# Meta tokens' values and the meta queries' turned block by one product of the whole array from masked copies

## The chip, the cores and the metric

One Trainium2 chip; the kernel runs on one of its cores. The metric is the device time of one execution in microseconds (us), as the median of the runs. On the core work TensorE (PE in the rows; its weight loads are PEld), VectorE (DVE), ScalarE (ACT) and GpSimd (POOL); SP issues the DMAs of the weights.

## What is computed

Two layers of a bidirectional encoder trunk. In front of the 256 tokens of the sequence stand 16 learned meta tokens. In each layer the input is normalised and projected; four token mixers of four heads each (A windowed attention with sinks, B rotary attention, C differential attention, D a gated linear recurrence in both directions) run side by side; their outputs are gated, merged, and a feed-forward block follows. Cut to the parts around the change:

```python
for l in range(DEPTH):
    u = rms_norm(h, ln_mix[l])
    (aq, ak, av, bq, bk, bv, cq, ck, cv, dq, dzf, dzb, di, dg, gz) = split_in(u @ w_in[l])
    y_a = windowed_sink_attention(aq, ak, av, attn_sink[l], bias_a)
    y_b = axial_rope_attention(rms_norm(bq, qk_norm_q[l]), rms_norm(bk, qk_norm_k[l]), bv, row, col, key_ok)
    y_c = differential_attention(cq, ck, cv, lam, bias_c, key_ok, diff_subnorm[l], lam_init)
    y_d = hgrn2_bidirectional(dq, dzf, dzb, di, dg, lb_all[0, l], lb_all[1, l], valid, hgrn_out_norm[l])
    gate = sigmoid(gz).reshape(Bn, L, N_BRANCH, D_MODEL)
    merged = sum(gate[:, :, n] * (y @ w_branch[l, n]) for n, y in enumerate((y_a, y_b, y_c, y_d)))
    h = h + merged @ w_out[l]
    u = rms_norm(h, ln_ffn[l])
    h = h + (silu(u @ w_ffn_gate[l]) * (u @ w_ffn_up[l])) @ w_ffn_down[l]
return rms_norm(h, ln_final)[:, META_END:]
```

Every mixer's output is, per head, weights (softmax or decayed scores) times values, over the meta tokens and the sequence. In the second layer only the sequence's outputs are needed, so the meta tokens are keys and values there, but not queries.

## The kernel before

Activations lie with features on the 128 partitions and the 272 tokens (16 meta, 256 of the sequence) along the free dimension. A projection to 128 features is a `block`: 24 matmuls (eight slices of the input, three products each of a value split in a high and a low fp32r part; L291 to L293) into one PSUM tile of the tag `pmm`. The weights stream through SP's queue, and ACT and DVE split each of them in two (L276, L277). The small products of the mixers are in f32, into PSUM tiles of the tag `pat`, of which there are four.

PE's order is written out by hand (`tc.manual_schedule`): the loop over `ORDER` runs one block after the other, and between blocks `catch_up` runs one step that was put off (`later`), and `advance` runs pieces of two generators, `branch_d` (mixer D) and `softmax_stream` (C, then B, then A). The order of the other engines is planned by the framework from the program's order and its own estimates of when operands are ready; each engine then runs its queue in order. A tile of a pool waits until the buffer that it gets is free.

What the change touches:
- `values` (L410) makes, from the projected values of a branch (features on partitions), `vn`, the sequence's values with tokens on the partitions (transposes, L417), and `vm`, the 16 meta tokens' values for four heads, each head on its own 32 partitions. For `vm` (L422 to L426) each head has a product of 64 contracted rows, 32 stationary columns (the meta tokens' columns, padded to 32) and 64 moving columns (`C_E`, an identity repeated in both halves). L427 masks the result. `take` (L938) puts `values` off to the next `catch_up`; for branch B `take_b` is put off first.
- `turn_meta` (L463) runs in layer 0 for C, B and A, one unit of the stream after the weights of the meta queries were made. Those lie as one tile of 128 partitions: 32 rows for each of the four heads, 272 keys along the free dimension. L467 turns the two halves of the sequence's keys; L470 turns the block of the meta keys, head by head, by four products of 32 rows and 32 columns with a piece of the identity.
- `mix` (L432) uses `vm` and the turned blocks. L443 and L437 are its products.
- L723 and L735 are the small products of `branch_d`; L402, L566, L393, L817 and L826 are small products that follow the block of `aq0` in layer 0; L460 is the transpose of the sequence queries' meta keys, by way of a copy in a tile of the tag `pmeta` (two buffers).
- `prep_small` (L158) works out four small parameters; `load_bias("a")` (L239 to L246) fills and masks a bias table from POOL's queue.

Of the kernel before, what the change touches and what calls it, by code (L numbers as in the profile page):

```python
# [8 lines left out]
F32 = mybir.dt.float32  # L9
# [3 lines left out]
ALU = mybir.AluOpType  # L13
AX = mybir.AxisListType

P = 128
# [4 lines left out]
T = META + SEQ  # L21
# [9 lines left out]
SWAP16 = list(range(16, 32)) + list(range(16))  # L31


C_ID, C_E, C_COS, C_SIN, C_SEL, C_RM, C_CM, C_EPS, C_ONE, C_WIDTH = (
    0, 128, 192, 464, 736, 738, 740, 742, 744, 872)
M_WIDTH = 5 * 32
Q_LNM, Q_LNF, Q_LNO, Q_SINK, Q_SINKM, Q_QK, Q_SUB, Q_OUT, Q_LAM, Q_LB, Q_WIDTH = (
    0, 16, 32, 40, 48, 50, 58, 60, 62, 318, 326)
# [36 lines left out]
def fap(t, p0, pn, off, dims):  # L75
    base = t[p0:p0 + pn]
    return bass.AP(tensor=base.tensor, offset=base.offset + off,
                   ap=[[base.ap[0][0], pn]] + [list(d) for d in dims])
# [3 lines left out]
def trunk(ctx, tc, xT, w_in, w_branch, w_out, w_gate, w_up, w_down, rel_bias, params, consts, masks, onehot, ln_out, out):  # L82
    nc = tc.nc
    V, S, G, PE = nc.vector, nc.scalar, nc.gpsimd, nc.tensor
    PE_ENGINE = mybir.EngineType.PE

    one = ctx.enter_context(tc.tile_pool(name="one", bufs=1))
# [10 lines left out]
    two = ctx.enter_context(tc.tile_pool(name="two", bufs=2))  # L98
# [43 lines left out]
    cst = one.tile([P, C_WIDTH], F32, name="cst")  # L142
# [14 lines left out]

    def prep_small():  # L158
        nc.sync.dma_start(out=par[:, Q_LAM:], in_=params[:, Q_LAM:])
        t = one.tile([P, 2, 2, 32], F32, name="lamt")  # L160
        s = one.tile([P, 2, 2], F32, name="lams")
        lp = par[:, Q_LAM:Q_LAM + 256].rearrange("p (l a d) -> p l a d", l=2, a=4)
        for l in range(2):
            V.tensor_tensor(out=t[:, l], in0=lp[:, l, 0::2, :], in1=lp[:, l, 1::2, :], op=ALU.mult)
        V.tensor_reduce(out=s.rearrange("p l a -> p (l a)"), in_=t.rearrange("p l a d -> p (l a) d"), axis=AX.X, op=ALU.add)
        S.activation(out=s.rearrange("p l a -> p (l a)"), in_=s.rearrange("p l a -> p (l a)"), func=AF.Exp)
        for l in range(2):
            li = 0.8 - 0.6 * math.exp(-0.3 * l)
            V.scalar_tensor_tensor(out=lam[:, l:l + 1], in0=s[:, l, 0:1], scalar=li, in1=s[:, l, 1:2],
                                   op0=ALU.add, op1=ALU.subtract)  # L170
            V.tensor_scalar(out=subg[:, l:l + 1], in0=par[:, Q_SUB + l:Q_SUB + l + 1], scalar1=1.0 - li,
                            scalar2=None, op0=ALU.mult)

        x = par[:, Q_LB:Q_LB + 8].rearrange("p (d e j) -> p d e j", d=2, e=2)
        m = one.tile([P, 2, 2], F32, name="lbm")
        e = one.tile([P, 2, 2, 2], F32, name="lbe")
        V.tensor_tensor(out=m, in0=x[:, :, 0, :], in1=x[:, :, 1, :], op=ALU.max)
        for d in range(2):
            V.tensor_tensor(out=e[:, :, d, :], in0=x[:, :, d, :], in1=m, op=ALU.subtract)
        ef = e.rearrange("p d e j -> p (d e j)")  # L180
        S.activation(out=ef, in_=ef, func=AF.Exp)
        V.tensor_tensor(out=m, in0=e[:, :, 0, :], in1=e[:, :, 1, :], op=ALU.add)
        mf = m.rearrange("p d j -> p (d j)")
        V.reciprocal(out=mf, in_=mf)
        for d in range(2):
            V.tensor_tensor(out=e[:, :, d, :], in0=e[:, :, d, :], in1=m, op=ALU.mult)
        lv = lb.rearrange("p (d j) -> p d j", d=2)
        V.tensor_tensor(out=lv, in0=e[:, :, 0, :], in1=e[:, :, 1, :], op=ALU.add)
        V.tensor_tensor(out=lv, in0=lv, in1=e[:, :, 0, :], op=ALU.subtract)
        V.tensor_scalar(out=lbc, in0=lb, scalar1=-1.0, scalar2=1.0, op0=ALU.mult, op1=ALU.add)  # L190
# [216 lines left out]
        return r  # L407


    def values(vts):  # L410

        n = len(vts)
        vn = (vpool if n == 1 else gl).tile([P, 2, n * P], F32, tag=f"vn{n}", name=nm("vn"))
        ps = pat()
        for i in range(2):
            for j in range(n):
                PE.transpose(ps[:, (i * n + j) * P:(i * n + j + 1) * P], vts[j][:, META + P * i:META + P * (i + 1)], ident)  # L417
        S.copy(vn.rearrange("p a b -> p (a b)"), ps[:, :2 * n * P])

        vm = vpool.tile([P, 2, 64], F32, tag="vm", name=nm("vm"))  # L420
        pm = pat()
        for hd in range(4):  # L422
            kv = hd // 2 if n == 1 else hd % 2
            vt = vts[0] if n == 1 else vts[hd // 2]
            r = slice(64 * kv, 64 * kv + 64)
            PE.matmul(pm[32 * hd:32 * hd + 32, :64], vt[r, 0:32], cst[r, C_E:C_E + 64], start=True, stop=True)  # L426
        V.tensor_tensor(out=vm, in0=fap(pm, 0, P, 0, [[0, 2], [1, 64]]), in1=fap(cst, 0, P, C_RM, [[1, 2], [0, 64]]), op=ALU.mult)  # L427
        return vn, vm.rearrange("p a b -> p (a b)")

# [30 lines left out]
        PE.transpose(ps[:, :P], pm.rearrange("p a b -> p (a b)"), ident)  # L460
        V.tensor_copy(pTm[:, q0:q0 + P], ps[:, :P])

    def turn_meta(p, pT, pTm):  # L463

        ps = pat()
        for i in range(2):
            PE.transpose(ps[:, i * P:(i + 1) * P], p[:, META + P * i:META + P * (i + 1)], ident)  # L467
        for hd in range(4):
            r = slice(32 * hd, 32 * hd + 32)
            PE.matmul(ps[r, 256:288], p[r, 0:32], cst[r, C_ID + 32 * hd:C_ID + 32 * hd + 32], start=True, stop=True,  # L470
                      tile_position=(32 * hd, 32 * hd))
        for i in range(2):
            V.tensor_copy(pT[i][:, :, 0:META], ps[:, i * P:(i + 1) * P].rearrange("p (a b) -> p a b", a=4)[:, :, :META])
        V.tensor_copy(pTm[:, 0:META], ps[:, 256:256 + META])
# [173 lines left out]
    def softmax_stream(l, c0, pj, done):  # L648

        makers = {2: parts_c, 1: parts_b, 0: parts_a}  # L650
        units = [(n, qt) for n in BRANCHES[1:] for qt in ((0, 1, None) if l == 0 else (0, 1))]
        state = {}
        pend = None

        def turned(u):
            n, qt, st = u
            if n not in state:
                state[n] = attn_out(l, c0)
            pT, pTm = state[n]
            if qt is not None:  # L660
                turn(st["p"], pT, pTm, qt)
            else:
                turn_meta(st["p"][:, 0, :], pT, pTm)
            yield
            if qt == units[-1][1]:
                vn, vm = pj["val", n]
                outs = mix(pT, pTm, vn, vm, c0, True)
                yield
                if n == 2:
                    g = post_c(l, c0, outs)  # L670
                    next(g)
                    yield
                    done[n] = next(g)
                else:
                    done[n] = [split_from(o, c0, yslot) for o in outs]

        for _ in range(WAIT_C[l]):
            yield
        for n, qt in units:
            while n == 1 and ("ready", 0) not in pj or ("ready", n) not in pj:  # L680
                yield
            if n == 1 and qt == 0:
                pj["a"] = parts_of(pj["aq"], pj["ak"])
            st = {}
            gen = makers[n](l, pj, qt, st)
            for k in range(2 if n == 2 else 1):
                next(gen)
                if n == 2 and k == 0:
                    yield
            next(gen, None)  # L690
            yield
            if pend:
                yield from turned(pend)
            pend = (n, qt, st)
        yield from turned(pend)


# [204 lines left out]
    for l in range(DEPTH):  # L902
# [19 lines left out]
        pj, done = {}, {}  # L922
        dt = {"T1": ptile(), "KK": ptile(), "q": slot(), "i": slot(), "g": slot()}
# [12 lines left out]
        later = []  # L936

        def take(n, tiles):  # L938
            def f():
                (dt if n == 3 else pj)["val", n] = values(tiles)  # L940
            later.append(f)

        def take_b():
# [8 lines left out]
        with tc.manual_schedule(engines={PE_ENGINE}):  # L952
            for idx, name in enumerate(ORDER):
                t0 = first_token(l, name)
                ps = lead[idx] if idx < 3 else block(acts, t0)
# [3 lines left out]
                if name[:2] == "dz":  # L959
                    d, j = name[2], int(name[3])  # L960
# [10 lines left out]
                    if l > 0:  # L971
                        c = 2 * dd + j
# [24 lines left out]
                if name[1] == "v":  # L997
                    n = "abc".index(name[0])
# [13 lines left out]
            for kind, i, m in MIXING if l < DEPTH - 1 else ():  # L1012
                n = BRANCHES[i]
                if kind == "g":
# [4 lines left out]
                    ps = block(acts, c0)  # L1019
# [11 lines left out]
                ps = pmm()  # L1031
# [5 lines left out]
                else:  # L1037
                    t = midt()
# [16 lines left out]
        for m in range(KT):  # L1055
            ps = pss[m] if l == DEPTH - 1 and m < 2 else block(merged, c0)
# [13 lines left out]
        for m in range(NFF):  # L1070
            if l == DEPTH - 1 and 4 <= m < 8:
                i, half = (m - 4) // 2, m % 2
                ps = pat()
# [22 lines left out]
        for m in range(KT):  # L1096
            ps = pmm()
# [17 lines left out]
    for i in range(2):  # L1115
        ss, r = col(2), col(1)
# [18 lines left out]
def _constants():  # L1135
# [3 lines left out]
    c = np.zeros((P, C_WIDTH), f)  # L1139
    p = np.arange(P)  # L1140
# [5 lines left out]
    d = p % 64  # L1146
# [5 lines left out]
    for n in range(5):  # L1152
        w = LEVELS[n]
        a, b = (p % 32)[:, None], np.arange(32)[None, :]
# [6 lines left out]
        c[:, C_CM + x] = (p // 32) % 2 == x  # L1161
    c[:, C_EPS] = EPS
    c[:, C_ONE:C_ONE + P] = 1.0

    rel = np.arange(RELS) - REL0
    half, exact = 16, 8
    n = np.abs(rel)
    nf = np.maximum(n, exact).astype(f)
    big = exact + (np.log(nf / f(exact)).astype(f) / f(math.log(128 / exact)) * f(half - exact)).astype(np.int32)
    b = np.where(rel > 0, half, 0) + np.where(n < exact, n, np.minimum(big, half - 1))  # L1170
# [92 lines left out]
```

## Time and profile before

| | us |
|---|---|
| median of 3 runs | 919.1 (918.74 to 919.21) |
| profiled execution, its own time | 920.86 |
| profiled execution, first to last instruction (span) | 919.1 |

The rows below come from the one profiled execution. In the rows of the order of time the start of each instruction in us from the span's start stands first, then how long it (or the run of xN alike) took, the engine and the line, what it wrote and read with the shapes, and in brackets the idle time of the engine ahead of it and what ended that. Matmuls overlap: the next one's start comes long before the end of the one before it, so the distance of starts tells the pace, and the length of one does not. "64*32" is the part of the array that a product uses, rows by columns.

### The profile page before, as it was taken

Reading aid. Unit: us, or ns where it says so; the run is one execution under the profiler, and the core shown is the slowest. Engines: PE = TensorE matmul, PEld = TensorE weight load, DVE = VectorE, ACT = ScalarE, POOL = GpSimd, SP = SyncE. Lnnn points to the kernel's source line nnn. Section 1 sums busy time; section 2 is a strip of 40 time slices with the busy share of each in tenths; the row PEclk is TensorE's granted clock in tenths of the full one; section 3 lists DMA queues with packets and bytes.
Section 4 is the critical chain, followed back from the end, with each engine's and each line's share of the span. In section 5 each row is a group of like instructions: output and inputs, shape, how many; then the busy total and the mean of one; then the engine's idle time right before and its main releaser. Section 6 shows DMA issues by size and latency. Waiting matters only on the chain.

```text
span 919.1 us, 18144 instructions
## 1 busy us (share of the span) xinstructions
PE 900.9 (98%) x7246; PEld 820.2 (89%) x7246; DVE 665.9 (72%) x1295; ACT 514.2 (56%) x898; POOL 25.8 (3%) x55
## 2 busy tenths in 40 slices
PE   7999999999999999999999999999999999999996
PEld 6998898989999999999999997777778988888885
DVE  6898686867887666675568997857767886667544
ACT  6655576664466444444446565767545666556443
POOL 1420000000000000000000000000000000000001
PEclk9998999999999999999999999999999999999999
DMA  8943334434555555555555433454365555555661
GB/s 302 249 158 103 106 124 130 138 116 140 174 175 175 174 171 181 168 179 180 168 181 163 160 119 117 149 174 155 115 200 153 182 178 183 187 186 191 192 184 46
DMA packets 42613, 150.01 MB, mean 163 GB/s; under 512 B 5024, under 2 KB 5696, under 8 KB 42528
## 3 DMA queue, kind: packets, MB, share of 16 engines
q1 hardware_dynamic: 40896, 144.84, 49.2%
q0 software_dynamic: 1344, 3.48, 1.5%
q8 instruction: 57, 0.93, 0.4%
q10 hardware_dynamic: 288, 0.52, 0.2%
q14 instruction: 28, 0.23, 0.1%
HBM read 147.22 MB, written 1.61 MB: 162 GB/s over the span
## 4 chain that ended last, share of the span: by engine, by line
PE 93%; DVE 4%; ACT 2%; issue 1%; DMA 1%; SPq 0%; ACTq 0%; DVEq 0%
PE pmm L291 18%; PE pmm L293 18%; PE pmm L292 18%; PE pmm L310 8%; PE pmm L319 6%; PE pmm L321 6%; PE pmm L320 6%; PE pmm L311 4%; PE pat L514 2%; PE pat L443 2%; PE pat L454 1%; PE pat L723 1%; DVE wlo L277 1%; DMA raw<-in_w_in_dram 1%; PE pat L437 1%
## 5 line engine op out<-in xcount | busy, mean ns | idle before, releaser
L276 ACT CAST whi<-raw 128x1024 fp32r<-128x1024 f32 (+1 forms) x275 | 285.2, 1039 | 309.9 <-PE pmm L292 141.9
L277 DVE TENSOR_TENSOR wlo<-raw,whi 128x1024 fp32r<-128x1024 f32 (+1 forms) x275 | 332.8, 1213 | 123.1 <-ACT whi L276 121.7
L291 PE MATMUL pmm<-slot,whi 128*128 128x272 f32 (+1 forms) x1232 | 361.1, 294 | 6.3 <-ACT slot L336 6.0
L293 PE MATMUL pmm<-slot,wlo 128*128 128x272 f32 (+1 forms) x1232 | 356.1, 289 | 0.9 <-DVE wlo L277 0.9
L292 PE MATMUL pmm<-slot,whi 128*128 128x272 f32 (+1 forms) x1232 | 356.5, 290 | 0.1
L291 PEld LDWEIGHTS pmm<-slot,whi 128*128 128x128 f32 x1232 | 234.0, 190 | 14.6 <-ACT slot L336 6.4
L292 PEld LDWEIGHTS pmm<-slot,whi 128*128 128x128 f32 x1232 | 235.1, 191 | 1.5 <-DVE slot L337 1.4
L293 PEld LDWEIGHTS pmm<-slot,wlo 128*128 128x128 f32 x1232 | 234.3, 190 | 1.7 <-DVE wlo L277 1.1
L310 PE MATMUL pmm<-slot,whi 128*128 128x512 f32 x320 | 112.5, 395 | 0.2 <-DVE mid L1081 0.2
L311 PE MATMUL pmm<-slot,wlo 128*128 128x256 f32 x320 | 89.8, 281 | 0.0
L319 PE MATMUL pmm<-whi,slot 128*128 128x512 f32 x184 | 73.6, 400 | 0.0
L310 PEld LDWEIGHTS pmm<-slot,whi 128*128 128x128 f32 x320 | 60.1, 188 | 14.4 <-ACT whi L276 0.4
L321 PE MATMUL pmm<-wlo,slot 128*128 128x512 f32 x184 | 72.9, 396 | 0.0
L320 PE MATMUL pmm<-whi,slot 128*128 128x512 f32 x184 | 72.1, 392 | 0.0
L311 PEld LDWEIGHTS pmm<-slot,wlo 128*128 128x128 f32 x320 | 60.2, 188 | 0.0
L319 PEld LDWEIGHTS pmm<-whi,slot 128*128 128x128 f32 x184 | 34.6, 188 | 9.9 <-issue 1.8
L320 PEld LDWEIGHTS pmm<-whi,slot 128*128 128x128 f32 x184 | 34.6, 188 | 7.7
L321 PEld LDWEIGHTS pmm<-wlo,slot 128*128 128x128 f32 x184 | 34.5, 188 | 7.6
L1081 DVE TENSOR_TENSOR mid<-pmm,rstd 128x272 f32<-128x272 f32 (+1 forms) x48 | 20.8, 440 | 24.7 <-PE pmm L293 24.6
L291 PE MATMUL pmm<-y,whi 128*128 128x272 f32 x128 | 37.1, 290 | 0.0
L293 PE MATMUL pmm<-y,wlo 128*128 128x272 f32 x128 | 36.9, 288 | 0.0
L292 PE MATMUL pmm<-y,whi 128*128 128x272 f32 x128 | 36.8, 288 | 0.0
(270 smaller groups left out, 1028.1 us busy)
## 6 DMA issues: line engine op xcount, KB each, us to landing
raw<-in_w_in_dram SPq DMA_DIRECT2D x106, 512.0 KB, 3.6
raw<-in_w_gate_dram SPq DMA_DIRECT2D x44, 512.0 KB, 3.6
raw<-in_w_up_dram SPq DMA_DIRECT2D x44, 512.0 KB, 3.5
raw<-in_w_down_dram SPq DMA_DIRECT2D x44, 512.0 KB, 3.7
raw<-in_w_branch_dram SPq DMA_DIRECT2D x16, 512.0 KB, 3.5
raw<-in_w_out_dram SPq DMA_DIRECT2D x16, 512.0 KB, 4.1
biasA<-scr POOLq DMA_DIRECT2D x8, 136.0 KB, 7.0
h<-in_xT_dram SPq DMA_DIRECT2D x3, 272.0 KB, 5.7
```

What stands on the lines that cost most here:

```text
L276: S.copy(hi[:, sl], raw[:, sl])
L277: V.tensor_tensor(out=lo[:, sl], in0=raw[:, sl], in1=hi[:, sl], op=ALU.subtract)
L291: PE.matmul(o, hi[:, sl], act[:, 0, c0:], start=first, stop=False)
L292: PE.matmul(o, hi[:, sl], act[:, 1, c0:], start=False, stop=False)
L293: PE.matmul(o, lo[:, sl], act[:, 0, c0:], start=False, stop=last)
L310: PE.matmul(ps[:, :2 * SEQ], hi[:, sl], acts[k][:, :, META:], start=k == 0, stop=False, skip_group_check=True)
L311: PE.matmul(ps[:, :SEQ], lo[:, sl], acts[k][:, 0, META:], start=False, stop=k == n - 1, skip_group_check=True)
L319: PE.matmul(o, a, hi[:, sl], start=first, stop=False)
L320: PE.matmul(o, b, hi[:, sl], start=False, stop=False)
L321: PE.matmul(o, a, lo[:, sl], start=False, stop=last)
L443: PE.matmul(ps[64 * hh:64 * hh + 64, c0:T], vn[:, i, vc:vc + 64], pT[i][:, hd, c0:], start=False, stop=i == 1, skip_group_check=True)
L1081: V.tensor_tensor(out=t[:, c0:], in0=ps[:, c0:T], in1=rstd[:, c0:], op=ALU.mult)
```

## The change

`values` gets a masked copy of the meta tokens' values, `spread`, made on POOL when the values have been projected (`take`): the 32 columns are repeated for the four heads, and the half of the partitions that isn't the head's own is set to zero. One product of 128 rows and 128 columns with the same `C_E` then gives all four heads. `turn_meta` gets `pd`, made on DVE right behind the weights (`diagonal`): the 32 columns of the meta keys repeated four times, with everything off the head's own block set to zero; one product with a matrix of four stacked identities of 32 (`C_E32`) turns it. Two constants are new (`C_S4`, `C_E32`, 36 columns), and `prep_small` takes its temporary from the `mid` pool.

```diff
-C_ID, C_E, C_COS, C_SIN, C_SEL, C_RM, C_CM, C_EPS, C_ONE, C_WIDTH = (
-    0, 128, 192, 464, 736, 738, 740, 742, 744, 872)
+C_ID, C_E, C_COS, C_SIN, C_SEL, C_RM, C_CM, C_EPS, C_ONE, C_S4, C_E32, C_WIDTH = (
+    0, 128, 192, 464, 736, 738, 740, 742, 744, 872, 876, 908)
...
-        t = one.tile([P, 2, 2, 32], F32, name="lamt")
+        t = midt()[:, :P].rearrange("p (l a d) -> p l a d", l=2, a=2)
...
-    def values(vts):
+    def spread_meta(vt, n):
+
+        t = two.tile([P, 4, 32], F32, tag="pmeta", name=nm("vspread"))
+        if n == 1:
+            src, sel = fap(vt, 0, P, 0, [[0, 2], [0, 2], [1, 32]]), fap(cst, 0, P, C_SEL, [[1, 2], [0, 2], [0, 32]])
+        else:
+            src, sel = fap(vt, 0, P, 0, [[T, 2], [0, 2], [1, 32]]), fap(cst, 0, P, C_SEL, [[0, 2], [1, 2], [0, 32]])
+        G.tensor_tensor(out=t.rearrange("p (a b) c -> p a b c", a=2), in0=src, in1=sel, op=ALU.mult)
+        return t.rearrange("p a b -> p (a b)")
+
+    def values(vts, spread):
...
-        for hd in range(4):
-            kv = hd // 2 if n == 1 else hd % 2
-            vt = vts[0] if n == 1 else vts[hd // 2]
-            r = slice(64 * kv, 64 * kv + 64)
-            PE.matmul(pm[32 * hd:32 * hd + 32, :64], vt[r, 0:32], cst[r, C_E:C_E + 64], start=True, stop=True)
+        PE.matmul(pm[:, :64], spread, cst[:, C_E:C_E + 64], start=True, stop=True)
...
-    def turn_meta(p, pT, pTm):
+    def diagonal(p):
+
+        t = two.tile([P, 4, 32], F32, tag="pmeta", name=nm("pd"))
+        V.tensor_tensor(out=t, in0=fap(p, 0, P, 0, [[0, 4], [1, 32]]), in1=fap(cst, 0, P, C_S4, [[1, 4], [0, 32]]), op=ALU.mult)
+        return t.rearrange("p a b -> p (a b)")
+
+    def turn_meta(p, pd, pT, pTm):
...
-        for hd in range(4):
-            r = slice(32 * hd, 32 * hd + 32)
-            PE.matmul(ps[r, 256:288], p[r, 0:32], cst[r, C_ID + 32 * hd:C_ID + 32 * hd + 32], start=True, stop=True,
-                      tile_position=(32 * hd, 32 * hd))
+        PE.matmul(ps[:, 256:288], pd, cst[:, C_E32:C_E32 + 32], start=True, stop=True)
...
-                turn_meta(st["p"][:, 0, :], pT, pTm)
+                turn_meta(st["p"][:, 0, :], st["pd"], pT, pTm)
...
             next(gen, None)
+            if qt is None:
+                st["pd"] = diagonal(st["p"])
             yield
...
         def take(n, tiles):
+            spread = spread_meta(tiles[0], len(tiles))
+
             def f():
-                (dt if n == 3 else pj)["val", n] = values(tiles)
+                (dt if n == 3 else pj)["val", n] = values(tiles, spread)
             later.append(f)
...
+    c[p, C_S4 + p // 32] = 1.0
+    c[p, C_E32 + p % 32] = 1.0
```

## Rows read from the trace of the kernel before

**Rows 1.** Page, busy time of each engine (share of span) and instructions.

```profile
PE 900.9 (98%) x7246; PEld 820.2 (89%) x7246; DVE 665.9 (72%) x1295; ACT 514.2 (56%) x898; POOL 25.8 (3%) x55
```

**Rows 2.** Table of stretches: busy us (instructions) per engine, PEclk, DMA share, GB/s.

```profile
78.00:83.00 5.00, 5.00 (x43) 4.73 (x43) 5.00 (x19) 2.26 (x4) 0.00 (x0) 1.00 0.35 112
...
88.40:93.40 5.00, 5.00 (x23) 4.96 (x23) 1.71 (x3) 0.35 (x1) 0.00 (x0) 0.50 0.33 105
...
546.00:551.00 5.00, 5.00 (x46) 4.16 (x45) 4.94 (x16) 3.76 (x7) 0.00 (x0) 1.00 0.30 107
```

**Rows 3.** Line L426: count, ns least/median/most, first and last start, forms.

```profile
L426 PE MATMUL pat<-cst,slot x64: 216/228/241, 57.8 to 566.0; 64*32 64x64 f32 x64
```

**Rows 4.** PE in order of time, one `turn_meta` (C, layer 0).

```profile
148.44 0.27 PE L467 MATMUL pat<-cst,p 128*128 128x128 f32 x1
...
149.07 0.29 PE L292 MATMUL pmm<-slot,whi 128*128 128x272 f32 x1
```

**Rows 5.** PE in order of time, small products of the whole array and what follows.

```profile
126.46 0.27 PE L460 MATMUL pat<-cst,pmeta 128*128 128x128 f32 x1
...
126.70 0.29 PE L292 MATMUL pmm<-slot,whi 128*128 128x272 f32 x1
...
83.17 0.95 PE L402 MATMUL pat<-cst,mid 128*128 128x2 f32 x8
...
83.87 0.25 PE L402 MATMUL pat<-cst,mid 128*128 128x2 f32 x1
84.05 0.21 PE L566 MATMUL pat<-cst,mid 64*32 64x1 f32 x4
...
483.68 0.25 PE L381 MATMUL pat<-cst,sq 128*128 128x1 f32 x1
...
484.00 0.29 PE L292 MATMUL pmm<-slot,whi 128*128 128x272 f32 x1
```

**Rows 6.** PE in order of time, `values` of A and of B, layer 0.

```profile
108.64 0.27 PE L417 MATMUL pat<-cst,slot 128*128 128x128 f32 x1
108.84 0.32 PE L426 MATMUL pat<-cst,slot 64*32 64x64 f32 x8
...
109.32 0.29 PE L292 MATMUL pmm<-slot,whi 128*128 128x272 f32 x1
...
93.90 0.27 PE L417 MATMUL pat<-cst,slot 128*128 128x128 f32 x1
...
94.35 0.50 PE L437 MATMUL pat<-ATm,vm 64*128 64x272 f32 x2
```

**Rows 7.** PE in order of time, `values` of C, then a run of L723 alone.

```profile
57.46 0.38 PE L417 MATMUL pat<-cst,slot 128*128 128x128 f32 x2
...
57.90 0.76 PE L723 MATMUL pat<-p,gk 64*32 64x32 f32 x60
...
61.99 0.74 PE L723 MATMUL pat<-p,gk 64*32 64x32 f32 x63
```

**Rows 8.** POOL's group of L1125; line L495; DVE in order of time.

```profile
L1125 POOL TENSOR_TENSOR hT<-hT,p 128x512 f32<-128x512 f32 x2 | 2.6, 1302 | 306.7 <-ACT p L1123 306.6
...
L495 DVE TENSOR_TENSOR y<-slot,y x6: 701/715/1576, 47.5 to 565.5; 128x544 fp32r<-128x544 f32 x6
...
47.49 1.58 DVE L495 TENSOR_TENSOR y<-slot,y 128x544 fp32r<-128x544 f32 x1
```

**Rows 9.** ACT and PE in order of time around L826, layer 0.

```profile
82.92 0.65 ACT L494 CAST y<-slot 128x544 fp32r<-128x544 f32 x1 [2.17 <-DVE slot L579]
...
84.53 1.28 ACT L405 ACT_TABLE_LOAD   x1
...
86.15 2.36 PE L826 MATMUL pat<-p,p 64*128 64x16 f32 x16 [0.69 <-ACT hr L405]
```

**Rows 10.** POOL's last selects of `load_bias("a")`; DVE's L988 of branch C.

```profile
48.45 3.89 POOL L246 TENSOR_SCALAR_AFFINE_SELECT biasAm<-biasAm 32x256 f32<-32x256 f32 x4
...
54.70 0.43 DVE L988 TENSOR_TENSOR slot<-pmm,rstd 128x272 f32<-128x272 f32 x1
```

## The prediction

> **What bounds the kernel now.** I read the page's busy times first, then the table of stretches, then TensorE start by start around the lines that the change touches. PE is busy for 98% of the span [rows 1], DVE for 72%, ACT for 56%, POOL for 3%. So a nanosecond that goes from PE's stream in the middle of the program is a nanosecond of the span, and work on DVE, ACT or POOL is free until PE has to wait for it. "Busy" does not mean well filled: what counts is the distance from one matmul's start to the next one's. [...]
>
> **What the change removes from PE.** `values` runs eight times (four branches, two layers), and each run has four partial products; every f32 product is two instructions, hence 64 on L426 [rows 3]. `turn_meta` runs three times (layer 0 only), which by the same count is 24 on L470. Together 88 instructions go and 11 products, 22 instructions, come.
>
> The busy times of those lines are no price, because the partial products run side by side. The price is the stretch that a site takes. In `turn_meta` the second transpose (L467) starts at 148.44 and the next block's second matmul (L292) at 149.07, so 0.63 us [rows 4]; I take L292 because the start that is recorded for L291 lies inside the matmul before it. A transpose with no partial products behind it reaches the same L292 in 0.24 us (126.46 to 126.70) [rows 5]. So the four products and what surrounds them cost 0.39 us.
>
> **What the new product costs on PE.** No row shows a full-array f32 product with 32 or 64 columns, so I bound it. The nearest are the L402 products of two columns: seven steps from 83.17 to 83.87, 0.10 us each, and the transposes of 128 columns, 0.11 us (the 0.38 us of two L417, less the 0.27 us of one) [rows 5 to 7]. So the new site is 0.11 (transpose) + 0.10 (first pass) + a tail from the second pass to L292. The tail is 0.24 us behind a product of 128 columns, and 0.32 us behind one of a single column (L381, 483.68 to 484.00) [rows 5]; 32 or 64 columns lie between, and I take 0.30. That makes 0.51 us, with bounds of 0.45 and 0.53. By sites:
> - `turn_meta`, three sites: 0.63 - 0.51 = 0.12 saved each, 0.36 in all (0.30 to 0.54).
> - `values` of the last branch, between full blocks: now 108.64 to 109.32, 0.68 us [rows 6]; 0.17 saved, and as much at its twin in layer 1: 0.34 (0.30 to 0.46).
> - `values` of branch B, followed by `mix`, which is itself in half-array tiles: now 93.90 to 94.35, 0.45 us [rows 6]. The step from a full small product to a tiled one is 0.18 us (L402 83.87 to L566 84.05) [rows 5], so 0.11 + 0.10 + 0.18 = 0.39: 0.06 saved, in both layers 0.12 (0 to 0.12).
> - `values` of branches C and D, followed by the many small L723 products: there the tiles of the two lines interleave. From the second L417 (57.46 + 0.11) to the end of the L723 run (57.90 + 0.76) it is 1.09 us now [rows 7]. A run of L723 alone takes 0.74 us from its first start to its end (61.99, 63 of its 64) [rows 7]. Afterwards: 0.39 to reach it, plus 0.74 or 0.75, 1.14. Here the change **loses** 0.05 each, 0.20 over four (0.10 to 0.40).
>
> Sum on PE: 0.36 + 0.34 + 0.12 - 0.20 = **0.62 us saved** (0.2 to 1.0).
>
> The row shows eight partial instructions of one site as a run of 0.32 us where one takes 0.23 [rows 3, 6], so they start within 0.1 us: no longer than two full passes. [...]
>
> **What is added elsewhere.** Three DVE products (`diagonal`) of 128x128: the subtraction of 128x544 on L495 has a median of 0.715 us [rows 8], a quarter is 0.18, with a start-up up to 0.3. They stand behind `normalise`, a whole unit of the softmax stream ahead of the transpose that uses them, and PE has no wait on DVE in that part. Cost nothing; uncovered, 0.3 each. The `pmeta` tag now has two users more, but all spreads of a layer are over before the first `turn`. The constants grow by 36 columns, 18 KB, and `lamt` moves into a `mid` buffer; both fall into the first 30 us. The first bound is nothing, the upper one 1.3 us, a table load more on ACT [rows 9], if the order there were planned differently; I take nothing.
>
> Eight POOL products (`spread_meta`). PE gets a new wait, for POOL; behind the waiting product stands PE's whole stream in the order written by hand, so a late spread costs the span what it is late. In layer 0 the POOL queue ahead of the first holds `load_bias("a")`, with its selects that wait for DMAs; its last selects run 48.45 to 52.34 us, and branch C's values are written at 54.70 to 55.13, while the product follows the transposes of 57.46 [rows 7, 10]. So POOL is free in time and has some 2 us; the other sites have a whole block of 24 matmuls as well. One spread: a POOL product of 128x512 took 1.30 us [rows 8], a quarter of that is 0.33; with a start-up I take 0.4 (0.3 to 0.9).
>
> POOL does cost DVE. While the selects ran, the subtraction of L495 that started at 47.49 took 1.58 us, more than twice the median [rows 8]. [...] Seven spreads fall where DVE has gaps or PE does not wait. One does not: branch B in layer 0. Its value (`bv`) is written early in the stretch from 78 to 83 us, of which DVE is busy for all 5.00 us [rows 2], through the rotary products until L579, for which ACT's L494 waits until 82.92; behind it in ACT's queue are L276 and the 1.28 us table load at 84.53, and only then does PE's L826 go on, at 86.15, with 0.69 us of idle time behind ACT [rows 9]. A spread there that blocks DVE for its 0.4 us moves all of that. I charge **0.4 us** (0 to 0.9).
>
> **Sum.** -0.62 + 0.4 = -0.2 us on the profiled execution's span of 919.1 us; its own time is 920.9, 1.8 us outside the span, untouched. The median of the runs is 919.1, and the same difference gives **918.9 us**. Likeliest case by its bounds: -1.0 to +0.7, 918.1 to 919.8.
>
> **Rivals.**
> - [...] Chance 0.19.
> - *The product gains nothing*. The full product's loads are not hidden behind 64 columns and cost what the packed ones did; POOL's 0.4 us stays: 919.5. Chance 0.12.
> - *The low clock goes.* The 5.00 us from 88.4 to 93.4 at 0.50 [rows 2] hold what takes 2.5 us at 1.00, and L826's 2.36 us ahead of them lie mostly in it too, some 0.8: 3.3 us less, 915.6. For it: the fall came right behind an idle time that the change can shift. Against: nothing in the change shortens that idle time. Chance 0.09.
> - *A second low stretch*, in layer 1's twin place: 3.3 us more, 922.2. Against: the products there only become fuller. Chance 0.08.
> - *The order of ACT and DVE comes out otherwise*, since the other engines' order is planned anew: one table load of 1.3 us more or less in a place where PE waits: 920.2 or 917.6, and with two loads, as likely, 921.5 or 916.3. For it: seven operations more on DVE and POOL in the first layer alone, and a buffer more in the `mid` ring. Against: none of them is late for anything. Chance 0.18.
>
> **How the numbers follow.** The forecast has 0.34, the rivals the chances above. About 0.2%, 1.84 us, is what a measurement of this kernel can tell from no change. Faster by more (below 917.3): the clock case 0.09 and the two loads fewer 0.05, 0.14. Slower by more (above 920.9): the second stretch 0.08 and the two loads more 0.05, 0.13. Same: 0.73. The range reaches to both ends of the planning case and leaves out the two clock cases, 0.17: 916.3 to 921.5.
>
> **What would show it.** Right: 16 instructions in place of L426's 64 and six in place of L470's 24; a `turn_meta` site of 0.45 to 0.53 us; the L723 sites no shorter than now; POOL products of 0.3 to 0.5 us; an idle time of PE ahead of L826 in layer 0 of some 1.1 us instead of 0.69. Wrong: a wait of PE for POOL at any site, a site with `mix` or L723 that is shorter by 0.1 or more, a changed number of half-clock stretches, or a gap of over 1 us somewhere that the change does not touch.

## The result, and the profile after

| | us |
|---|---|
| before, median of 5 runs beside the changed kernel | 919.1 (916.29 to 921.25) |
| changed kernel, median of 5 runs | 925.6 (922.96 to 927.44) |
| ratio | 1.0065 (95% interval 1.005 to 1.008) |
| profiled execution of the changed kernel, its own time | 927.44, span 925.7 |

The changed kernel is slower by some 0.65%, 6.5 us. The forecast was 918.9, with a range of 916.3 to 921.5, so the time lies outside it, and slower by over 0.2% had been given a chance of 0.13. The page's first lines after hardly differ from [rows 1]: PE does 66 instructions fewer, DVE three more, POOL eight more, and PE's share falls from 98 to 97%.

```profile
span 925.7 us, 18035 instructions
PE 901.9 (97%) x7180; PEld 822.8 (89%) x7180; DVE 668.2 (72%) x1298; ACT 514.0 (56%) x898; POOL 31.2 (3%) x63
```

What shows the loss is the list of PE's waits (engine, tile and line that waited, what ended the wait; us in total, times, longest). Its second line has no counterpart in the same list of the kernel before, where no wait on `pmeta` stands:

```profile
PE pmm L291 <- ACT slot L336: 5.4, 2, 4.7
PE pat L466 <- DVE pmeta L464: 4.7, 2, 2.5
PE pmm L293 <- DVE wlo L277: 1.9, 2, 1.0
```

L466 (L460 before) is the transpose at the end of `turn` and reads the small copy `pmeta` that DVE makes on L464 (L458 before). Twice, for the second half of C's queries and of A's in layer 0, PE stands still, for 2.5 and 2.3 us. The first of them in order of time, PE, then ACT, then DVE, and at the end PE's second wait:

```profile
140.33 0.27 PE L460 MATMUL pat<-cst,p 128*128 128x128 f32 x1
143.08 0.30 PE L466 MATMUL pat<-cst,pmeta 128*128 128x128 f32 x1 [2.48 <-DVE pmeta L464]
...
139.69 1.05 ACT L276 CAST whi<-raw 128x1024 fp32r<-128x1024 f32 x1 [0.78 <-ACT p L626]
140.64 0.52 ACT L490 ACTIVATE p<-p,col 128x272 f32<-128x272 f32 x1
...
140.77 1.23 DVE L277 TENSOR_TENSOR wlo<-raw,whi 128x1024 fp32r<-128x1024 f32 x1 [0.34 <-ACT whi L276]
141.91 0.28 DVE L472 TENSOR_TENSOR pd<-p,cst 128x128 f32<-128x128 f32 x1
142.11 0.68 DVE L462 COPY pT<-pat 128x512 f32<-128x512 f32 x1
142.71 0.22 DVE L464 COPY pmeta<-p 128x128 f32<-128x128 f32 x1
...
216.36 0.47 PE L466 MATMUL pat<-cst,pmeta 128*128 128x128 f32 x1 [2.26 <-DVE pmeta L464]
```

DVE's rows are best read from the last one back. The copy that PE waits for (L464) stands behind `pd` (L472), the new product of the change. `pd` needs the normalised weights of the meta queries (L490, ready at 141.16), and ahead of it in DVE's queue is a weight split that waits for ACT. In the kernel before, the same copy was made 7 us ahead of its transpose (which started at 141.06):

```profile
133.94 0.22 DVE L458 COPY pmeta<-p 128x128 f32<-128x128 f32 x1
```

It is the same in all three branches. From this copy to its transpose there were 7.1 us in C, 3.5 in B and 5.0 in A before; in the changed kernel 0.4, 0.4 and 0.3 are left, and PE waits 2.48, 0.09 and 2.26 us.

Behind each of the two waits of the profiled execution the granted clock falls to 0.50 for some 3.4 us. In the table of stretches (columns as in [rows 2]):

```profile
139.00:144.40 5.40, 2.92 (x25) 2.72 (x25) 3.81 (x11) 2.26 (x4) 0.00 (x0) 1.00 0.54 168
144.40:147.80 3.40, 3.40 (x16) 3.18 (x15) 0.00 (x0) 0.05 (x1) 0.00 (x0) 0.50 0.12 47
147.80:152.00 4.20, 4.20 (x38) 4.02 (x38) 3.34 (x10) 3.69 (x10) 0.00 (x0) 1.00 0.00 0
213.00:216.10 3.10, 1.10 (x10) 0.86 (x9) 2.63 (x7) 2.56 (x7) 0.00 (x0) 1.00 0.74 251
216.10:219.50 3.40, 3.14 (x14) 3.14 (x15) 1.38 (x5) 0.00 (x0) 0.00 (x0) 0.50 0.45 164
```

**Where the 6.6 us between the two spans are.** PE's matmuls stand in the same order in both kernels apart from the replaced products, so each has a partner, and the difference of their starts can be followed through the program:

| piece of the program (us in the kernel before) | change of the difference, us |
|---|---|
| start to 17.3 | -1.04 |
| 17.3 to 86.2: sites of C and D, POOL's part at L826, ahead of them a wait (L723, near 52 us) that grew by 0.2 | +0.69 |
| 86.2 to 109.1: sites of B and A, layer 0 | -0.25 |
| wait at 141.1 | +2.61 |
| half clock behind it | +1.55 |
| wait at 177.9 (B) | +0.24 |
| wait at 210.4 | +2.42 |
| half clock behind it | +1.45 |
| three `turn_meta` sites | -0.45 |
| layer 1 and the rest | -0.64 |
| sum | +6.58 |

The first piece is the start of these two executions (the matmuls of the first block go on at half pace, some 6 a us against 10 later, until about 11 instead of 15 us), not the change. Of the last piece, -0.24 is A's site in layer 1, and -0.38 falls between 750 and 850 us, where the change touches nothing: e7_ring_only below, which has the products of the kernel before, shows -0.39 there too. The two long waits and the clock behind them are 8.0 us; everything else together is below zero.

### The profile page after: what moved, and what is told of

Its sections match the earlier page's. It is cut to its first block, busy times and chain, and to the rows that moved or that the text cites. A ratio compares the mean times of both kernels' runs of the same rounds, so it can differ in the third digit from the quotient of the medians.

```text
span 925.7 us, 18035 instructions
## 1 busy us (share of the span) xinstructions
PE 901.9 (97%) x7180; PEld 822.8 (89%) x7180; DVE 668.2 (72%) x1298; ACT 514.0 (56%) x898; POOL 31.2 (3%) x63
## 4 chain that ended last, share of the span: by engine, by line
PE 91%; DVE 5%; ACT 2%; issue 1%; DMA 1%; SPq 0%; ACTq 0%; DVEq 0%
PE pmm L291 18%; PE pmm L293 17%; PE pmm L292 17%; PE pmm L310 8%; PE pmm L319 6%; PE pmm L321 6%; PE pmm L320 6%; PE pmm L311 4%; PE pat L523 2%; PE pat L449 2%; DVE wlo L277 1%; PE pat L460 1%; ACT whi L276 1%; PE pat L734 1%; PE pat L443 1%
```

## The experiments

The question is why the copies that ran 3.5 to 7 us early now run late. Three theories:
- *Hand-out order.* The ring `pmeta` gives its buffers to tiles in the order of the program. `pd` comes ahead of that copy in the program, so the copy can't be placed on DVE before `pd` is.
- *Program order, or shortage.* DVE follows the program's order anyway, whatever the ring (this is the second theory of the expectations); or two buffers are too few for `pd` and the copies.
- *POOL.* The eight spreads on POOL block DVE, and that makes the copies late.

**pd in a buffer of its own** (e1_own):

```diff
+    pd_own = one.tile([P, P], F32, name="pdown")
...
-        rb16 = one.tile([32, 16, 8], F32, name="rb16")
+        rb16 = pd_own[:32, :].rearrange("p (a b) -> p a b", a=16)
...
-        t = two.tile([P, 4, 32], F32, tag="pmeta", name=nm("pd"))
+        t = pd_own.rearrange("p (a b) -> p a b", a=4)
```

> The changed kernel, but pd has a buffer of its own (128 columns that an early small tile also uses) and is out of the pmeta ring; its place in the program stays ahead of the pmeta copy of the unit before. First theory (the ring hands its buffers out in the order of the program, so that copy can't be placed on DVE ahead of pd, and PE's transpose waits for it): both waits of over 2 us (transpose of C and of A, layer 0) are gone, and so are the half-clock stretches behind them; the copies of C and A come several us ahead of their transposes again; span some 0.5 to 1 us below the kernel before, 918.2 to 919. Second theory (DVE simply follows the program's order, pd first): nothing changes, some 925. Third theory (the POOL products block DVE, and that makes it late): the waits stay, since all eight POOL products stay.

Measured: 918.2 (median of 12) against 918.9 (median of 23), ratio 0.9994 (0.9981 to 1.0008). PE has no wait on `pmeta` any more. Of the half-clock stretches only the one from 88 us on and the one at the program's end are left; every profile has these two. In order of time, DVE's copy, PE's transpose, and `pd`:

```profile
132.36 0.22 DVE L466 COPY pmeta<-p 128x128 f32<-128x128 f32 x1
...
139.48 0.27 PE L468 MATMUL pat<-cst,pmeta 128*128 128x128 f32 x1
...
140.95 0.29 DVE L474 TENSOR_TENSOR pdown<-p,cst 128x128 f32<-128x128 f32 x1
```

The copy is 7 us early again (B's 3.5 and A's 5.1), though `pd` still comes first in the program; `pd` itself runs as late as it did. So program order alone is not it, nor is POOL, whose eight products are all there. The time itself can't tell this kernel from the one before.

**Three buffers in the ring** (e4_ring3):

```diff
+    pmr = ctx.enter_context(tc.tile_pool(name="pmr", bufs=3))
...
-        t = two.tile([P, 4, 32], F32, tag="pmeta", name=nm("pd"))
+        t = pmr.tile([P, 4, 32], F32, tag="pmeta", name=nm("pd"))
```

(The spreads' tile and the copy's tile likewise; the early small tile `rb16` goes to the `mid` pool.)

> The changed kernel with three buffers in the pmeta ring in place of two (an early small tile moves to another pool to make room). If the ring was too short, the two waits go and the time falls to about 918.5. First theory (buffers are handed out in the order of the program, however many there are): the copy still stands behind pd on DVE, both waits of 2 to 3 us and the half-clock stretches stay, 924 to 927.

Measured: 924.6 (median of 4), ratio 1.0065 (1.0041 to 1.0089): all of the loss. DVE's order is that of the changed kernel, `pd` and right behind it the copies:

```profile
139.99 0.28 DVE L473 TENSOR_TENSOR pd<-p,cst 128x128 f32<-128x128 f32 x1
140.19 0.68 DVE L463 COPY pT<-pat 128x512 f32<-128x512 f32 x1
140.79 0.21 DVE L465 COPY pmeta<-p 128x128 f32<-128x128 f32 x1
```

So it is no shortage of buffers. This execution also splits the loss in two: behind the first wait the clock fell, behind the second it did not.

```profile
PE pat L467 <- DVE pmeta L465: 4.7, 2, 2.5
...
142.30:145.60 3.30, 3.30 (x17) 3.30 (x16) 0.00 (x0) 0.00 (x0) 0.00 (x0) 0.50 0.15 60
214.40:217.80 3.40, 3.36 (x27) 3.36 (x28) 2.44 (x7) 0.12 (x1) 0.00 (x0) 1.00 0.52 167
```

17 matmuls fit in 3.30 us at 0.50, and 27 in 3.40 us at 1.00. The wait is there each time; the low clock stood behind one of them and not behind the other.

**pd one place later in the program, in the same ring of two** (e2_late):

```diff
-            if qt is None:
-                st["pd"] = diagonal(st["p"])
             yield
             if pend:
                 yield from turned(pend)
+            if qt is None:
+                st["pd"] = diagonal(st["p"])
```

> The changed kernel with pd in the pmeta ring of two as it is, but made (and taken from the ring) after the turn of the unit before instead of ahead of it: one place later in the program, the same operations. If the order of the hand-outs is the cause, the copy of the unit before gets its buffer first, both waits go, and the time is that of the run with pd's own buffer, some 918 to 919. If sharing the two buffers with pd is the cause in itself, the waits stay, 924 to 927.

Measured: 919.0, ratio 0.9992 (0.9979 to 1.0005); no wait on the copy is left, and DVE makes it ahead of `pd` again, 7.1 us before its transpose:

```profile
133.21 0.22 DVE L464 COPY pmeta<-p 128x128 f32<-128x128 f32 x1
...
142.61 0.28 DVE L472 TENSOR_TENSOR pd<-p,cst 128x128 f32<-128x128 f32 x1
```

So the shared ring does no harm by itself; the place in the hand-out does. (How the framework plans is not recorded; that it goes by the hand-out is the one theory left of the three.) One thing came that was not expected: with `pd` that late, A's product waits for `pd` once, 1.3 us, because DVE has the branch merging of that stretch ahead of it:

```profile
PE pat L480 <- DVE pd L472: 1.3, 1, 1.3
...
216.50 0.43 DVE L1052 SCALAR_TENSOR_TENSOR mid<-slot,pmm 128x272 f32<-128x272 f32 x1
216.85 0.28 DVE L472 TENSOR_TENSOR pd<-p,cst 128x128 f32<-128x128 f32 x1
```

**The two halves of the change, each alone** (e5_values has no `pd` and the four partial products in `turn_meta`; e6_turn has no spread and the four partial products in `values`):

```diff
 e5_values
-            if qt is None:
-                st["pd"] = diagonal(st["p"])
...
 e6_turn
-            spread = spread_meta(tiles[0], len(tiles))
...
```

> Only the half of the change in values: eight POOL spreads and one product each; turn_meta has its four partial products as before, and there is no pd. First theory: no wait on pmeta; the sites of values save 0.2 us on PE in all (A twice 0.22, B twice 0.08, C and D some 0.4 lost), and POOL costs 0.1 to 0.2 us ahead of the products that follow the block of aq0: 918.8 to 919.3. Third theory (POOL): the time stays above 923.

> Only the half in turn_meta: pd by DVE in the pmeta ring of two and one product; values has its four partial products and no spread. First theory: the two waits and the half-clock stretches are all there, 924 to 927, some 0.2 us off the changed kernel. Third theory (POOL): 918.6.

Measured: the half in `values` 919.4, 0.1 us above what was expected, ratio 1.0002 (0.9989 to 1.0014); the half in `turn_meta` 925.1, ratio 1.0064 (1.0038 to 1.0089, median of 4), with the wait on `pmeta` of 4.7 us in two pieces. The whole loss belongs to the second half, and POOL is not in it.

**The wait without the product** (e7_ring_only): the products of the kernel before (`values` as in e6_turn), and only DVE's `pd` in the ring, which nobody reads.

```diff
-        PE.matmul(ps[:, 256:288], pd, cst[:, C_E32:C_E32 + 32], start=True, stop=True)
+        for hd in range(4):
+            r = slice(32 * hd, 32 * hd + 32)
+            PE.matmul(ps[r, 256:288], p[r, 0:32], cst[r, C_ID + 32 * hd:C_ID + 32 * hd + 32], start=True, stop=True,
+                      tile_position=(32 * hd, 32 * hd))
...
```

> The kernel before, with nothing new but pd: DVE makes it in the pmeta ring at the place of the change, and no product uses it; values and turn_meta have their partial products as before (the constants and the mid buffer for the early temporary are those of the change). If the wait is all of the loss, this one costs what the changed kernel costs and the 0.7 us more that its PE sites do not save: 925 to 928. If the new product has a part in the loss, it is nearer to 919.

Measured: 926.4 (median of 4; beside it, e2_late and the two kernels below, the kernel before ran at 919.8, median of 29), ratio 1.0062 (1.0042 to 1.0082). Three DVE products of 0.284 us whose result nobody reads cost all of it. The line of PE's waits is the same as in the changed kernel:

```profile
PE pat L470 <- DVE pmeta L468: 4.7, 2, 2.5
```

**What is left when the wait is gone.** Two kernels built on pd's own buffer: one uses the whole-array product of `values` for branch A alone and has a spread for A alone (e8_a_only); the other makes all spreads on DVE (e9_dve).

```diff
 e8_a_only
-            spread = spread_meta(tiles[0], len(tiles))
+            spread = spread_meta(tiles[0], len(tiles)) if n == 0 else None
...
 e9_dve
-        G.tensor_tensor(out=t.rearrange("p (a b) c -> p a b c", a=2), in0=src, in1=sel, op=ALU.mult)
+        V.tensor_tensor(out=t.rearrange("p (a b) c -> p a b c", a=2), in0=src, in1=sel, op=ALU.mult)
```

> pd in its own buffer; the whole-array product of values only for branch A, where full blocks stand on both sides; branches B, C and D keep their four partial products and have no POOL spread. By the sites: turn_meta 3 x 0.16 and A 0.22 + 0.23 saved, 0.9 us; no POOL product ahead of the products that follow the block of aq0, so PE's gap there is 1.07 us as before and not 1.21. Some 918.0, 0.1% below the kernel before, which this measurement may not tell from none.

> pd in its own buffer, and the eight spreads made by DVE instead of POOL. [...] Where branch B's spread lies in the chain in layer 0, PE's gap ahead of the products after the block of aq0 grows from 1.07 us (before) to about 1.35, against 1.21 with POOL; elsewhere nothing. 918.5 to 919.5.

Measured: branch A alone 918.0, ratio 0.9978 (0.9965 to 0.9991); spreads on DVE 918.7, ratio 0.9983 (0.9970 to 0.9996). Both intervals lie just below 1, so both kernels are faster than the one before, by 0.2%. Whether they are faster than e1_own (0.9994, against other runs of the kernel before) is not shown: the intervals overlap. What their expectations turn on is the idle time of PE ahead of the products that follow `aq0`'s block in layer 0 (L826 before): first e8_a_only, then e1_own, then e9_dve.

```profile
85.39 0.94 PE L845 MATMUL pat<-p,p 64*128 64x16 f32 x6 [0.69 <-ACT hr L407]
...
86.41 1.53 PE L839 MATMUL pat<-p,p 64*128 64x16 f32 x16 [0.83 <-ACT hr L407]
...
85.35 1.53 PE L839 MATMUL pat<-p,p 64*128 64x16 f32 x16 [0.89 <-ACT hr L407]
```

0.69 as in [rows 9] without a spread for B, 0.14 more with POOL's, 0.20 more with DVE's. (The expectations count from the start of the last product ahead of the gap: that way it is 1.07, 1.21 and 1.27 us, where 1.35 had been expected for the last: 1.07 and the 0.28 us that DVE took for `pd`, L472.)

## Why the prediction was wrong

**The step that failed** is the one on the three DVE products: "They stand behind `normalise`, a whole unit of the softmax stream ahead of the transpose that uses them, and PE has no wait on DVE in that part. Cost nothing". It looked at who reads `pd` and how early `pd` is, and that was right: the product of `turn_meta` never waited for it in the changed kernel. It did not ask what stands behind `pd`, in DVE's queue and in the ring. There stands the copy for the turn of the unit before, with PE's transpose of that copy directly behind it. "The `pmeta` tag now has two users more, but all spreads of a layer are over before the first `turn`" names the ring, and settles it for the spreads only; `pd` is the other user, and it lies between two copies of one branch. In [rows 1] and in the waits of before nothing pointed at `pmeta`, because its copies had been made 3.5 to 7 us early; that lead was the cover, and the change took it away. The term put at nothing measured +5.3 us of waits (2.61, 0.24 and 2.42 in the table above) and some 1.5 us for each low stretch of the clock behind one. Two of the prediction's own signs of being wrong came: the number of half-clock stretches changed, and gaps of over 1 us stand at a transpose that the change does not touch.

**The rival on the planned order** came nearest to what happened (another order on DVE, planned anew), but as a chance event with the price of table loads; its "none of them is late for anything" is the same oversight. *A second low stretch* was given a chance for layer 1's twin place; the stretches came behind the new waits in layer 0.

**The sum on PE was right in its direction at each kind of site, and its terms were a little off.** The sites of the changed kernel in order of time:

```profile
152.00 0.27 PE L479 MATMUL pat<-cst,p 128*128 128x128 f32 x1
152.11 0.31 PE L480 MATMUL pat<-cst,pd 128*128 128x32 f32 x2
...
152.46 0.29 PE L292 MATMUL pmm<-slot,whi 128*128 128x272 f32 x1
...
108.23 0.27 PE L427 MATMUL pat<-cst,slot 128*128 128x128 f32 x1
108.34 0.33 PE L432 MATMUL pat<-cst,vspread 128*128 128x64 f32 x2
...
108.70 0.29 PE L292 MATMUL pmm<-slot,whi 128*128 128x272 f32 x1
...
93.56 0.27 PE L427 MATMUL pat<-cst,slot 128*128 128x128 f32 x1
...
93.94 0.50 PE L443 MATMUL pat<-ATm,vm 64*128 64x272 f32 x2
...
56.66 0.38 PE L427 MATMUL pat<-cst,slot 128*128 128x128 f32 x2
...
57.13 0.76 PE L734 MATMUL pat<-p,gk 64*32 64x32 f32 x64
58.10 0.25 PE L746 MATMUL pat<-p,gk 64*32 64x16 f32 x8 [0.21 <-ACT vn L428]
```

| site | before | forecast | after |
|---|---|---|---|
| `turn_meta` [rows 4] | 0.63 | 0.51 | 0.46 |
| `values` of A, layer 0 [rows 6] | 0.68 | 0.51 | 0.47 |
| `values` of B, layer 0 [rows 6] | 0.45 | 0.39 | 0.38 |
| `values` of C, layer 0, to the end of the small products [rows 7] | 1.09 | 1.14 | 1.13 |

The term that was mis-sized is the step between the two passes: taken as 0.10 us from L402, it is 0.06 us at 64 columns and 0.03 us at 32, from one recorded start to the next. (The 0.10 was itself a mean of unlike steps: of the seven on L402 one is 0.03 us and six are 0.11.) The direction held at each kind of site: a gain between full products and ahead of `mix`, a small loss where the many small L723 products follow. C in layer 0 lost more than its row says: behind the small products PE waits 0.21 us for ACT's copy `vn`, which it did not before, and by the next block 0.29 us are gone, against 0.01 to 0.03 at the other three sites of C and D and 0.05 in the forecast. By the difference of starts all sites together save some 0.7 us, this wait counted, against 0.62 in the sum. What causes the wait was not tested; it is no price of the product alone, since e6_turn and e8_a_only, which keep the four partial products in C, wait there for 0.4 us. Branch A alone has the lowest ratio of the kernels measured, as the sites would have it, but its interval does not set it apart from e1_own and e9_dve.

**POOL's part was over-priced.** A spread took 0.40 us at the least, as estimated, and 1.01 at the most. Below the group stand the spread of B in layer 0, then a DVE instruction that ran beside it, then the same one in the kernel before:

```profile
L417 POOL TENSOR_TENSOR vspread<-slot,cst x8: 400/456/1011, 54.6 to 569.6; 128x128 f32<-128x128 f32 x8
...
78.99 1.01 POOL L417 TENSOR_TENSOR vspread<-slot,cst 128x128 f32<-128x128 f32 x1 [16.48 <-DVE slot L1001]
...
79.66 0.41 DVE L821 TENSOR_SCALAR p<-p,tot 128x128 f32<-128x128 f32 x1
...
80.15 0.27 DVE L810 TENSOR_SCALAR p<-p,tot 128x128 f32<-128x128 f32 x1
```

The spread of branch B in layer 0 ran into DVE's chain as foreseen, but it was POOL that lost most of the time there: the spread took 0.6 us longer than the shortest one, and of DVE's instructions beside it only this one took longer, by 0.14 us. PE's idle time ahead of L826 grew by the same 0.14 us, not by 0.4. The 0.4 us charged in the sum takes DVE to stand still for the whole spread; that was the author's estimate, and no run shows it. PE waited for POOL nowhere, as argued from POOL's queue.

Without the one wait the time agrees with the forecast: with pd's own buffer the ratio is 0.9994, where the working gave 918.9/919.1 = 0.9998. That does not confirm the sum, since the interval (0.9981 to 1.0008) holds no change as well as a gain of 1.7 us; the rows of the sites are the evidence for it.

## What to carry to other kernels

When a tile joins a ring that others use, find the tiles that come next to it in the program: if buffers are handed out in that order, a tile whose data come late holds back the one behind it, however early that one's data are ready; here it did so with two buffers and with three, 4.7 us of PE's waits each time. A new operation is costed not by its own reader alone, but by what stands behind it in its queue and in its ring, and by how early those ran before. And an engine that never shows up as a wait may be quiet only because of a lead, which a profile of before shows as the distance from a copy to its reader (here 3.5 to 7.1 us).

## What had not been expected of the hardware

A wait of PE of 2.3 to 2.5 us was followed by a stretch of 3.4 us at a granted clock of 0.50 in six of the eight cases that the four profiles with such waits show (changed kernel twice, e6_turn twice, e4_ring3 once of two, e7_ring_only once of two; the case behind the second wait is missing in the last two). Over each such stretch the distance to the kernel before grew by some 1.5 us more, over half of what the wait itself cost.

The length of the wait alone does not decide it. An idle time of 0.7 to 0.9 us near 86 us was followed by a low stretch in all ten profiles; one of 0.6 to 1.4 us near 52 us only in e5_values (1.44 us, the longest there); the 1.3 us of e2_late by none. What does decide it stays open. The low stretch near 86 us also differs in length: 6.8 us in six profiles, the kernel before and the changed one among them, and 3.4 us in e1_own, e4_ring3, e5_values and e9_dve. The sixteen products behind that idle time (L826 before) took 2.36 us in the kernel before and 2.30 in the changed one, but 1.53 in e1_own and in e9_dve. By the two half-clock pieces of the table above (1.55 and 1.45), the shorter stretch alone takes some 1.5 us off the profiled span of e1_own (916.3 against 919.1), which is why the kernels are compared by their medians here.
